# Rotating the place of the weight pairs inside their buffers, in a two-layer encoder trunk

## The chip, the cores and the metric

The kernel runs on one core of a Trainium2 chip. The metric is the device time of one execution in microseconds (us). Two runs of the kernel before took 1237.33 and 1236.85 us; their median is 1237.09 us.

## The reference

The kernel computes a small encoder trunk of depth 2 on one sequence of 512 frames with 1024 features, in float32:

```python
for layer in range(DEPTH):
    mod = c_act @ mod_w[layer] + mod_b[layer]
    sh1, sc1, g1, sh2, sc2, g2 = jnp.split(mod, N_MOD, axis=-1)
    u = modulate(rms_norm(h, norm_mix[layer]), sh1, sc1)
    if layer < N_A_LAYERS:
        mix = hgrn2_mixer(u, a_w_in[layer], a_w_out[layer], lower_bounds[layer], a_out_norm[layer])
    else:
        j = layer - N_A_LAYERS
        mix = chunk_band_attention(u, k_pad, v_pad, b_w_q[j], b_w_o[j], b_rel_bias[j])
    h = h + g1[:, None, :] * mix
    u = modulate(rms_norm(h, norm_ffn[layer]), sh2, sc2)
    h = h + g2[:, None, :] * swiglu(u, ffn_w_in[layer], ffn_w_out[layer])
    if layer == N_A_LAYERS - 1:
        k_pad, v_pad = shared_kv(h, c_act, kv_norm, kv_mod_w, kv_mod_b, kv_w)
return rms_norm(h, final_norm)
```

Layer 0 mixes with a gated linear recurrence of 8 heads, layer 1 with a band attention of 16 heads; each layer ends with a feed-forward part, `swiglu(u) = (silu(u @ gate) * (u @ up)) @ w_out`, whose inner width is 2816. All large products have a weight matrix from memory on one side and the activations of the 512 frames on the other.

## The kernel before, in words

**Precision by pairs.** A large product is done in the reduced format `float32r`. Each operand is split into a high part (a rounded copy, made by ScalarE) and a low part (the operand less its high part, made by VectorE), and three matmuls are added up in PSUM: high by high, high weight by low input, low weight by high input. `mm3` (L187) does this for one block of 128 by 128 weights, L190 to L192. TensorE loads the 128 weight columns first (LDWEIGHTS, "PEld" in the profile, while the matmul before is still running) and then streams the 512 or 256 columns of the other operand past them. So there is one weight load for each matmul.

**The weights' way.** `load` (L146) reads a block of weights, 1024 floats in each of 128 partitions, by a DMA on the SP queue into a buffer of the tag `raw`. `fetch` and `split` (L123) make the pair `wh`, `wl` out of it, one block ahead of its use. The pool `wp` has three buffers for each tag, and a buffer of the tags `wh` and `wl` is as long as the longest tile that asks for one: 64 + 1024 floats, 4352 bytes. `SHIFT` (L54) is the 64. Four blocks (the two weights of tile 3 of each feed-forward part) get their low part from ScalarE and an adding DMA on the POOL queue instead (L130, L131).

**Where the operands lie.** In the kernel before, a pair made by `split` starts at the head of its buffers, and so do the eight first pairs made by `high` (L653). In the allocation of the kernel before, the heads of all six `wh` and `wl` buffers lie 192 bytes above a multiple of 256 (the first at byte 66,240), and so do the split activations (`u0h` at 20,928, the inputs of the fast tiles at 128,960 or 120,768, with every later tile a multiple of 256 bytes further). So a weight row (512 bytes) that is loaded for `mm3` starts at distance 0 modulo 256 bytes from the row that is streaming. "Distance" below is this one: of the weights loaded from the row that streams, modulo 256 bytes.

**The fast tiles.** In both feed-forward parts the first four of the 22 inner tiles go through `mm3` with 512 streamed columns. The other 18 (`fast_tiles`, L515) are done by a scheme with seven products of half-sized blocks in place of eight, on sums and differences of weights and inputs. `prepare` makes four pairs for each tile, with `halves` (L520): the pairs of `w1`, `w2`, `w3` hold two operands of 512 floats each, `w4` holds one. `product` (L553) then does 4 by 3 matmuls of 256 streamed columns, at L558 (high, high), L559 (high weight, low input) and L560 (low weight, high input). That is 84 matmuls for a tile and 3,024 for 36 tiles. These pairs do not start at the head:

```python
wh, wl = (wp.tile([P, SHIFT + D], F32R, tag="w" + x, name=f"{key}_{x}")[:, NEAR:NEAR + 4 * n_ * P]
          .rearrange("p (i j c) -> p i j c", i=n_, j=4) for x in "hl")
```

`NEAR` is 48 floats, so they lie at distance 192.

**The other weight products.** Outside the fast tiles, 8 first pairs with 18 matmuls each, 82 pairs with 24, and the 16 output rows of the feed-forward parts (three pairs, 22 blocks, 66 matmuls each) make 144 + 1,968 + 1,056 = 3,168 matmuls. The very last row streams its 512 frames as two halves of 256 columns, so there are 3,102 of 512 and 132 of 256 columns. All of them load at distance 0. (In the value projections, L213 to L215, the weights are streamed and the activations are loaded.)

**Order.** Each engine works its queue in order; semaphores are set by the tile framework. TensorE's order is the order of the program: the weight products fill in around the small products of the recurrence and of the attention. The change does not touch any of this.

Of the kernel before, what the change touches and what calls it, by code (L numbers as in the profile page):

```python
# [10 lines left out]
F32R = mybir.dt.float32r  # L11
# [4 lines left out]
P = 128  # L16
D = 1024
# [33 lines left out]

SHIFT, NEAR = 64, 48  # L54


V1_AFTER, CREDIT, RATES = 1, 3.0, (3.5, 16, 2.0, 56, 1.5)
# [12 lines left out]
def trunk(ctx: ExitStack, tc: tile.TileContext, d, out):  # L70
# [4 lines left out]
    wp = ctx.enter_context(tc.tile_pool(name="wp", bufs=3))  # L75
# [3 lines left out]
    def bank(name):  # L79
        return pp.tile([P, S], F32, tag="ps", name=name)  # L80
# [6 lines left out]
    h = [cst.tile([P, S], F32, tag=f"h{j}", name=f"h{j}") for j in range(KT)]  # L87
# [28 lines left out]
    V.tensor_mul(cact, cols[:, C_C:C_C + KT], csig)  # L116


    def by_transfer(key):

        return key[0] in [f"f{layer}" for layer in FAST] and key[1] == PLAIN - 1

    def split(raw, nk, n, nm, tag, key):  # L123
        wh = wp.tile([P, nk, n], F32R, tag=tag + "h", name=f"{nm}_h")
        wl = wp.tile([P, nk, n], F32R, tag=tag + "l", name=f"{nm}_l")
        A.activation(wh, raw, AF.Copy)  # L126

        state.pop("meanwhile", lambda: None)()
        if by_transfer(key):
            A.activation(wl, raw, AF.Copy, scale=-1.0)  # L130
            G.dma_start(out=wl, in_=raw, accum_op=ALU.add)  # L131
        else:
            low = V.tensor_sub(wl, raw, wh)  # L133
            if key[0] in ("av", "g", "zf", "q", "ao") or key[1] == "o":
                state["mods_after"] = low
        return wh, wl
# [2 lines left out]
    plan = weight_plan(d)  # L139
    ready = {}  # L140
    shifts, partial = {}, {}
    state = {"loaded": 0, "split": 0, "used": 0}
    raws = {}
    LOAD_AHEAD, SPLIT_AHEAD = 2, 1

# [8 lines left out]
    def fetch(i, ahead):  # L154
        load(i + LOAD_AHEAD + 1)
        if i + ahead + 1 < len(plan) and by_transfer(plan[i + ahead + 1][0]):
            ahead += 1
        while state["split"] < min(i + ahead + 1, len(plan)) and plan[state["split"]][0][-1] not in ("c1", "c2"):
            key, _, nk, n = plan[state["split"]]
            nm = "_".join(str(x) for x in key)  # L160
            raw = raws.pop(key)
            ready[key] = split(raw, nk, n, nm, "w", key)
            if key in shifts:

                sh = shifts[key]
                pa = sm.tile([P, S], F32, tag="et", name=f"wsh_{nm}", bufs=2)[:, 0:P]
                V.tensor_scalar_mul(pa, raw[:, 0, :], sh[:, 0:1])
                for kt in range(1, nk):
                    V.scalar_tensor_tensor(pa, raw[:, kt, :], sh[:, kt:kt + 1], pa, op0=ALU.mult, op1=ALU.add)
                partial[key] = pa  # L170
            state["split"] += 1

    def weight(key, ahead=SPLIT_AHEAD):
        assert plan[state["used"]][0] == key, (plan[state["used"]][0], key)
        fetch(state["used"], ahead)
        state["used"] += 1
        return ready.pop(key)

    def take(key):

        assert plan[state["used"]][0] == key, (plan[state["used"]][0], key)
        load(state["used"] + LOAD_AHEAD + 1)
        state["used"] += 1
        state["split"] = state["used"]
        return raws.pop(key)
# [329 lines left out]
    def fast_tiles(fp, nm, slot, activated, kept, side):  # L515

        H = S // 2
        ops = {}

        def halves(key, raw, n_):  # L520
            wh, wl = (wp.tile([P, SHIFT + D], F32R, tag="w" + x, name=f"{key}_{x}")[:, NEAR:NEAR + 4 * n_ * P]
                      .rearrange("p (i j c) -> p i j c", i=n_, j=4) for x in "hl")
            A.activation(wh, raw, AF.Copy)  # L523
            V.tensor_sub(wl, raw, wh)  # L524
            return [(wh[:, i], wl[:, i]) for i in range(n_)]

        def prepare(n):

            m = f"{nm}_{n}"
            c1 = take((nm, n, "c1")).rearrange("p (o j) c -> p o j c", o=2)  # L530
            c2 = take((nm, n, "c2")).rearrange("p (o j) c -> p o j c", o=2)
            x1 = fp.tile([P, 2, 4, P], F32, tag="x1", name=f"{m}_x1")
            x2 = fp.tile([P, 2, 4, P], F32, tag="x2", name=f"{m}_x2")
            b11, b21, b22, b12 = c1[:, 0], c1[:, 1], c2[:, 0], c2[:, 1]
            t2, t1, t3, t4 = x1[:, 0], x1[:, 1], x2[:, 0], x2[:, 1]
            ops[n, 1], ops[n, 2] = halves(f"{m}_w1", c1, 2)
            V.tensor_sub(t1, b12, b11)
            V.tensor_sub(t2, b22, t1)
            yield
            ops[n, 6], ops[n, 5] = halves(f"{m}_w2", x1, 2)  # L540
            V.tensor_sub(t3, b22, b12)
            V.tensor_sub(t4, b21, t2)
            yield
            ops[n, 7], ops[n, 4] = halves(f"{m}_w3", x2, 2)
            yield
            ops[n, 3], = halves(f"{m}_w4", c2[:, 0:1], 1)
            yield

        def stream():
            for n in range(PLAIN, FT):  # L550
                yield from prepare(n)

        def product(n, i, ps, s, start, stop):  # L553
            wh, wl = ops.pop((n, i))
            for j in range(4):
                uh, ul = slot(j, s)
                f = start and j == 0
                T.matmul(ps, wh[:, j, :], uh, start=f, stop=False, skip_group_check=True)  # L558
                T.matmul(ps, wh[:, j, :], ul, start=False, stop=False, skip_group_check=True)  # L559
                T.matmul(ps, wl[:, j, :], uh, start=False, stop=stop and j == 3, skip_group_check=True)  # L560

        chunks = stream()
        done = {"n": 0}

        def ahead(upto):
            while done["n"] < upto and next(chunks, chunks) is not chunks:
                done["n"] += 1

        AHEAD = 2
        for i, n in enumerate(range(PLAIN, FT)):  # L570
            at = activated(n)
            r1, r2, r3 = (bank(f"{nm}_r{q}_{n}")[:, 0:H] for q in (1, 2, 3))
            pu = sm.tile([P, 2, H], F32, tag="ut", name=f"{nm}_pu{n}", bufs=2)
            qu = sm.tile([P, 2, H], F32, tag="et", name=f"{nm}_qu{n}", bufs=2)
            p1, u2, p5, u3 = pu[:, 0, :], pu[:, 1, :], qu[:, 0, :], qu[:, 1, :]
            row1, row2 = at[:, H:S], at[:, 0:H]

            ahead(4 * i + 1 + AHEAD)
            product(n, 1, r1, 1, True, True)
            A.activation(p1, r1, AF.Copy)  # L580
            product(n, 5, r2, 4, True, True)
            A.activation(p5, r2, AF.Copy)
            ahead(4 * i + 2 + AHEAD)
            product(n, 6, r1, 5, False, True)
            A.activation(u2, r1, AF.Copy)
            product(n, 2, r3, 3, True, True)
            V.tensor_add(p1, r3, p1)
            A.activation(p1, p1, AF.Silu)
            ahead(4 * i + 3 + AHEAD)
            product(n, 7, r1, 6, False, True)  # L590
            A.activation(u3, r1, AF.Copy)
            ahead(4 * i + 4 + AHEAD)
            product(n, 3, r2, 7, False, True)
            V.tensor_add(row2, u3, p5)
            V.tensor_add(row1, r2, u2)
            V.tensor_mul(row1, row1, p1)
            product(n, 4, r1, 2, False, True)
            A.activation(p5, r1, AF.Silu)
            last = V.tensor_mul(row2, row2, p5)
            kept(n, at)  # L600
            if i % 3:
                state["mods_after"] = last
                next(side, None)
        state["mods_after"] = last
        fetch(state["used"] - 1, 1)
# [11 lines left out]
    first = [bank(f"first{i}") for i in range(6)]  # L617
    fraw, mrow, wfs, u, sqs, a1 = {}, {}, {}, {}, {}, []
# [32 lines left out]
        return r  # L651

    def high(j):  # L653
        wfs[j] = [wp.tile([P, 6, P], F32R, tag="w" + x, name=f"first{j}_{x}") for x in "hl"]
        A.activation(wfs[j][0], fraw[j], AF.Copy)

    def low(j):
# [312 lines left out]
    with tc.manual_schedule():  # L970
# [21 lines left out]
        A.activation(crow[:, S:S + 256], pcs[1][:, 0:256], AF.Copy)  # L992
        V.tensor_copy(crow[:, S + 256:D], pcs[1][:, 256:S])
        high(0)
        a1.append(mod_entry(0, 1))
        rounded(0)
# [126 lines left out]
    for n in range(2):  # L1123
        w, ps = weight(("ao", n)), bank(f"ao_{n}")
# [11 lines left out]
    for n in range(KT):  # L1136
        if n < len(part):
            w, ps = part[n]
# [36 lines left out]
    with tc.tile_pool(name="attn", bufs=1) as ap:  # L1175
# [146 lines left out]
        for k in range(len(units) + LAG2 + 1):  # L1322
            if k < len(units):
                hd, i = units[k]
# [20 lines left out]
        for n in range(KT):  # L1345
            if n < len(part):
                w, ps = part[n]
# [219 lines left out]
```

## Time and profile before

| what | value |
|---|---|
| median of 2 runs | 1237.09 us |
| span of the profiled execution | 1235.1 us |
| TensorE matmuls busy | 1219.8 us, 8548 instructions |
| TensorE weight loads busy | 1061.0 us, 8548 instructions |
| VectorE busy | 987.8 us |
| ScalarE busy | 648.8 us |
| matmuls of the fast tiles | 3 groups of 1008 |

The span runs from the first to the last instruction of the profiled execution. No time of its own beside the span is shown for that execution; the median of the runs is 2.0 us above its span, and this is taken for what lies around it. A matmul's duration in the profile is longer than the distance to the next one's start, because matmuls overlap in the array. What a matmul costs in a dense stretch is the time from its start to the start of the next.

### The profile page before, as it was taken

To read this page: it belongs to the slowest core of one execution; us is meant where nothing else is said; L and a number is where in the kernel's file an instruction comes from. 1 tells how busy PE (TensorE), PEld (TensorE's weight loads), DVE (VectorE), ACT (ScalarE), POOL (GpSimd) and SP (SyncE) were. 2 spreads that over 40 slices of the span, in tenths; PEclk is the share of its full clock that TensorE was granted. 3 is DMA by queue.
4 is the path that set the end of the run, shared out by engine and by line. 5 is a ranking of instruction groups with operands and counts; after the bars stand their busy time and mean duration, and the time that the engine had idled before them with its cause. 6 is when DMAs were issued, how large, how long until landed. Compare 5 with 4: busy or idle time off the path is not lost.

```text
span 1235.1 us, 21555 instructions
## 1 busy us (share of the span) xinstructions
PE 1219.8 (99%) x8548; PEld 1061.0 (86%) x8548; DVE 987.8 (80%) x1769; ACT 648.8 (53%) x1157; POOL 21.4 (2%) x29
## 2 busy tenths in 40 slices
PE   8999999999999999999999999999999999999997
PEld 7888788778899999988888877777889999998887
DVE  8996878887989999987669878996788999984333
ACT  6455446444655555742228566675465555563221
POOL 0100000000000000000000000000000000000000
PEclk9999999999999999999999999999999999999999
DMA  9642345553434444568752444532243444342331
GB/s 353 254 133 88 123 170 164 172 192 106 123 114 140 137 137 140 164 210 277 233 168 71 140 147 152 172 100 68 69 134 106 137 137 137 103 129 94 96 92 68
DMA packets 52532, 177.55 MB, mean 144 GB/s; under 512 B 5968, under 2 KB 8400, under 8 KB 52432
## 3 DMA queue, kind: packets, MB, share of 16 engines
q1 hardware_dynamic: 51856, 174.08, 43.1%
q0 software_dynamic: 576, 2.10, 1.0%
q8 instruction: 67, 1.10, 0.4%
q14 instruction: 33, 0.27, 0.1%
HBM read 171.96 MB, written 2.10 MB: 141 GB/s over the span
## 4 chain that ended last, share of the span: by engine, by line
PE 90%; DVE 5%; ACT 3%; issue 1%; DMA 1%; POOL 0%; DVEq 0%; POOLq 0%; ACTq 0%
PE f_r L560 10%; PE f_r L559 9%; PE f_r L558 9%; PE f_o L191 6%; PE f_o L192 6%; PE f_o L190 6%; PE f L190 2%; PE f L192 2%; PE f L191 2%; PE o L858 1%; PE bo L1270 1%; PE bo L190 1%; PE av L213 1%; PE bo L192 1%; PE bo L191 1%; PE ao L192 1%
## 5 line engine op out<-in xcount | busy, mean ns | idle before, releaser
L560 PE MATMUL f_r<-f_h,f_w_l 128*128 128x256 f32 x1008 | 282.3, 280 | 0.0
L558 PE MATMUL f_r<-f_h,f_w_h 128*128 128x256 f32 x1008 | 281.2, 279 | 0.0
L559 PE MATMUL f_r<-f_l,f_w_h 128*128 128x256 f32 x1008 | 281.2, 279 | 0.0
L559 PEld LDWEIGHTS f_r<-f_l,f_w_h 128*128 128x128 f32 x1008 | 189.5, 188 | 0.1
L560 PEld LDWEIGHTS f_r<-f_h,f_w_l 128*128 128x128 f32 x1008 | 189.2, 188 | 0.0
L558 PEld LDWEIGHTS f_r<-f_h,f_w_h 128*128 128x128 f32 x1008 | 188.5, 187 | 0.1
L191 PE MATMUL f_o<-f_p,f_o_h 128*128 128x512 f32 (+1 forms) x374 | 141.1, 377 | 0.3 <-DVE f_p L475 0.3
L192 PE MATMUL f_o<-f_p,f_o_l 128*128 128x512 f32 (+1 forms) x374 | 141.2, 378 | 0.0
L190 PE MATMUL f_o<-f_p,f_o_h 128*128 128x512 f32 (+1 forms) x374 | 140.8, 377 | 0.0
L126 ACT ACTIVATE f_o_h<-r_f_o 128x1024 fp32r<-128x1024 f32 (+1 forms) x48 | 46.8, 987 | 131.9 <-PE f_o L191 101.3
L340 DVE SCALAR_TENSOR_TENSOR mw<-mw,crow 128x1024 f32<-128x1024 f32 x96 | 115.4, 1218 | 0.7 <-DMA mw<-in_modw 0.6
L133 DVE TENSOR_TENSOR f_o_l<-r_f_o,f_o_h 128x1024 fp32r<-128x1024 f32 (+1 forms) x48 | 54.1, 1132 | 68.0 <-ACT f_o_h L126 60.4
L523 ACT ACTIVATE f_w_h<-f_x 128x1024 fp32r<-128x1024 f32 x72 | 76.5, 1063 | 49.1 <-PE f_r L559 42.0
L524 DVE TENSOR_TENSOR f_w_l<-f_x,f_w_h 128x1024 fp32r<-128x1024 f32 x72 | 88.0, 1225 | 8.7 <-ACT f_w_h L523 4.0
L523 ACT ACTIVATE f_w_h<-r_f_c 128x1024 fp32r<-128x1024 f32 x72 | 61.1, 848 | 49.5 <-PE f_r L559 48.1
L192 PEld LDWEIGHTS f_o<-f_p,f_o_l 128*128 128x128 f32 x374 | 70.3, 188 | 14.1 <-DVE f_o_l L133 1.4
L191 PEld LDWEIGHTS f_o<-f_p,f_o_h 128*128 128x128 f32 x374 | 70.4, 188 | 13.5 <-DVE f_p L475 0.7
L190 PEld LDWEIGHTS f_o<-f_p,f_o_h 128*128 128x128 f32 x374 | 70.4, 188 | 12.9
L524 DVE TENSOR_TENSOR f_w_l<-r_f_c,f_w_h 128x1024 fp32r<-128x1024 f32 x72 | 68.6, 952 | 7.7 <-ACT f_w_h L523 7.5
L1245 ACT ACTIVATE sb<-sb,st 128x128 f32<-128x128 f32 (+1 forms) x64 | 35.8, 560 | 29.9 <-DVE st L1244 29.4
L761 DVE TENSOR_TENSOR kq<-kq,t 128x1024 f32<-128x1024 f32 x28 | 34.2, 1220 | 5.2 <-PE fine L785 2.7
L192 PE MATMUL f<-f_h,f_l 128*128 128x512 f32 x96 | 36.9, 391 | 0.0
(401 smaller groups left out, 2706.3 us busy)
## 6 DMA issues: line engine op xcount, KB each, us to landing
mw<-in_modw SPq DMA_DIRECT2D x96, 512.0 KB, 4.2
r_f_c<-in_ffn_in SPq DMA_DIRECT2D x72, 512.0 KB, 3.5
r_f_o<-in_ffn_out SPq DMA_DIRECT2D x32, 512.0 KB, 3.6
mrow<-in_modw SPq DMA_DIRECT2D x16, 512.0 KB, 8.2
r_f<-in_ffn_in SPq DMA_DIRECT2D x16, 512.0 KB, 3.5
r_f_o<-in_ffn_out SPq DMA_DIRECT2D x16, 384.0 KB, 3.4
r_av<-in_a_v SPq DMA_DIRECT2D x8, 512.0 KB, 4.1
r_g<-in_a_g SPq DMA_DIRECT2D x8, 512.0 KB, 3.3
```

The source lines that it names most:

```text
L126: A.activation(wh, raw, AF.Copy)
L133: low = V.tensor_sub(wl, raw, wh)
L190: T.matmul(ps, wh[:, kt, :], uh, start=start, stop=False)
L191: T.matmul(ps, wh[:, kt, :], ul, start=False, stop=False)
L192: T.matmul(ps, wl[:, kt, :], uh, start=False, stop=stop)
L340: V.scalar_tensor_tensor(mw, mw, 1.0, crow, op0=ALU.mult, op1=ALU.mult, accum_out=raw[:, j:j + 1])
L523: A.activation(wh, raw, AF.Copy)
L524: V.tensor_sub(wl, raw, wh)
L558: T.matmul(ps, wh[:, j, :], uh, start=f, stop=False, skip_group_check=True)
L559: T.matmul(ps, wh[:, j, :], ul, start=False, stop=False, skip_group_check=True)
L560: T.matmul(ps, wl[:, j, :], uh, start=False, stop=stop and j == 3, skip_group_check=True)
L1245: A.activation(s[:, 0:n], s[:, 0:n], AF.Exp, bias=st[:, 1:2], accum_out=st[:, 2:3])
```

## The change

All pairs of weights, from `split`, from `halves` and from `high`, now come from one helper, `placed`. It takes a whole buffer of 64 + 1024 floats and hands out a part of it that starts 0, 8, 16, ... 56 floats behind the head: 0 to 224 bytes in steps of 32. A counter goes up by one for each half of a pair, so the high and the low part of one pair lie at the same distance, and the next pair lies 32 bytes further, in the order in which pairs are made. The number of instructions, their order, the sizes of the buffers and the waits are as before.

```diff
-SHIFT, NEAR = 64, 48
+SHIFT, STEP = 64, 8
...
+    def placed(name, tag, nk, n):
+        t = wp.tile([P, SHIFT + D], F32R, tag=tag, name=name)
+        at = STEP * (state["placed"] // 2 % (SHIFT // STEP))
+        state["placed"] += 1
+        return t[:, at:at + nk * n].rearrange("p (k c) -> p k c", k=nk)
...
     def split(raw, nk, n, nm, tag, key):
-        wh = wp.tile([P, nk, n], F32R, tag=tag + "h", name=f"{nm}_h")
-        wl = wp.tile([P, nk, n], F32R, tag=tag + "l", name=f"{nm}_l")
+        wh, wl = (placed(f"{nm}_{x}", tag + x, nk, n) for x in "hl")
...
-    state = {"loaded": 0, "split": 0, "used": 0}
+    state = {"loaded": 0, "split": 0, "used": 0, "placed": 0}
...
         def halves(key, raw, n_):
-            wh, wl = (wp.tile([P, SHIFT + D], F32R, tag="w" + x, name=f"{key}_{x}")[:, NEAR:NEAR + 4 * n_ * P]
-                      .rearrange("p (i j c) -> p i j c", i=n_, j=4) for x in "hl")
+            wh, wl = (placed(f"{key}_{x}", "w" + x, 4 * n_, P).rearrange("p (i j) c -> p i j c", i=n_) for x in "hl")
...
     def high(j):
-        wfs[j] = [wp.tile([P, 6, P], F32R, tag="w" + x, name=f"first{j}_{x}") for x in "hl"]
+        wfs[j] = [placed(f"first{j}_{x}", "w" + x, 6, P) for x in "hl"]
```

Fifty pairs are made before the first fast tile of layer 0 (8 first, 8 and 10 and 8 and 8 of the mixer, 8 of the plain tiles) and 186 before that of layer 1, both 2 more than a multiple of 8. So in both layers the fast tiles alternate between the distances 64, 96, 128, 160 and 192, 224, 0, 32 for their four pairs. The first three pairs of a tile serve 24 matmuls each and the fourth 12, so of the 3,024 matmuls 432 load at each of 0, 64, 96, 128, 192 and 224 bytes, and 216 at each of 32 and 160. The other weight products spread evenly over the eight.

## The prediction

> **What bounds the kernel now.** I read the page first: the busy times, then the chain that ended last.
>
> ```profile
> span 1235.1 us, 21555 instructions
> ...
> PE 1219.8 (99%) x8548; PEld 1061.0 (86%) x8548; DVE 987.8 (80%) x1769; ACT 648.8 (53%) x1157; POOL 21.4 (2%) x29
> ...
> PEclk9999999999999999999999999999999999999999
> ...
> PE 90%; DVE 5%; ACT 3%; issue 1%; DMA 1%; POOL 0%; DVEq 0%; POOLq 0%; ACTq 0%
> ```
>
> TensorE works all the time at full granted clock, and nine tenths of the chain are its matmuls. The time is the sum of start-to-start distances of matmuls, so the change can act only through these, or through another engine made so slow that it becomes late. Next the groups of instructions, kept apart by shape, for the matmuls that the change touches:
>
> ```profile
> L560 PE MATMUL f_r<-f_h,f_w_l 128*128 128x256 f32 x1008 | 282.3, 280 | 0.0
> L558 PE MATMUL f_r<-f_h,f_w_h 128*128 128x256 f32 x1008 | 281.2, 279 | 0.0
> L559 PE MATMUL f_r<-f_l,f_w_h 128*128 128x256 f32 x1008 | 281.2, 279 | 0.0
> ...
> L191 PE MATMUL f_o<-f_p,f_o_h 128*128 128x512 f32 x330 | 128.6, 390 | 0.3 <-DVE f_p L475 0.3
> ...
> L191 PE MATMUL f_o<-f_p,f_o_h 128*128 128x256 f32 x44 | 12.5, 285 | 0.0
> ```
>
> The same shape, 256 streamed columns, lasts 279 ns in the fast tiles, where weights lie at distance 192, and 285 ns in the last output row, where they lie at distance 0. To see what that is worth I took the order of time on TensorE in three dense stretches, first and last of equal steps:
>
> ```profile
> 341.82 0.28 PE L560 MATMUL f_r<-f_h,f_w_l 128*128 128x256 f32 x1
> ...
> 348.89 0.28 PE L560 MATMUL f_r<-f_h,f_w_l 128*128 128x256 f32 x1
> ```
>
> ```profile
> 1209.79 0.28 PE L190 MATMUL f_o<-f_p,f_o_h 128*128 128x256 f32 x1
> ...
> 1218.43 0.28 PE L190 MATMUL f_o<-f_p,f_o_h 128*128 128x256 f32 x1
> ```
>
> ```profile
> 599.71 0.39 PE L191 MATMUL f_o<-f_p,f_o_h 128*128 128x512 f32 x1
> ...
> 605.83 0.39 PE L191 MATMUL f_o<-f_p,f_o_h 128*128 128x512 f32 x1
> ```
>
> Sixty steps of 256 columns at distance 192 take 7.07 us, 117.8 ns each. Seventy-two steps of 256 columns at distance 0 take 8.64 us, 120.0 ns each. Twenty-seven steps of 512 columns at distance 0 take 6.12 us, 226.7 ns each. At distance 0, 256 more columns cost 226.7 - 120.0 = 106.7 ns, so 256 columns alone take 106.7 ns, and 13.3 ns come on top of each matmul whatever its length: the price of its weight load at distance 0. At distance 192 that price is 117.8 - 106.7 = 11.1 ns. So the trace shows one effect of place, of 2.2 ns, at two of the eight distances.
>
> **The change, part by part.** Nothing is removed or added: instructions, waits, DMAs and their order are the same. What moves is the distance.
>
> The fast tiles, 3,024 matmuls: 432 go to distance 0 and pay 2.2 ns more, 0.95 us. 432 stay at 192 and change by nothing. The other 2,160 load at distances that no row shows. The nearest rows are the two that I have; I take the middle between them, 118.9 ns, as nothing draws it to either: 2,160 x 1.1 ns = 2.4 us. Between the ends, like 192 or like 0, this is 0 to 4.75 us. Beyond both ends, a gain or a loss is not excluded; the rivals price it.
>
> The 3,102 matmuls of 512 columns: 388 stay at distance 0. 2,714 leave it. Two places in the trace have a 512-column matmul while a load at distance 192 runs, the last before the fast tiles of each layer:
>
> ```profile
> 339.95 0.39 PE L192 MATMUL f<-f_h,f_l 128*128 128x512 f32 x1
> 340.17 0.28 PE L558 MATMUL f_r<-f_h,f_w_h 128*128 128x256 f32 x1
> ```
>
> ```profile
> 925.48 0.39 PE L192 MATMUL f<-f_h,f_l 128*128 128x512 f32 x1
> 925.71 0.28 PE L558 MATMUL f_r<-f_h,f_w_h 128*128 128x256 f32 x1
> ```
>
> They take 0.22 and 0.23 us, mean 0.225 against 0.2267, which with times rounded to 10 ns speaks for a small gain, not for a large one. The ends are no gain and the 2.2 ns of the shorter matmuls, 0 to 6.0 us. I take 0.5 ns, nearer to no gain, since the mean over the seven distances lies between none (if like 0) and what 192 gives, which those two rows hold small: -1.4 us. The 132 half-width matmuls of the last row gain 1.1 ns in seven of eight: -0.1 us.
>
> The writers of the pairs, ScalarE and VectorE, now write and read at other places:
>
> ```profile
> L523 ACT ACTIVATE f_w_h<-f_x 128x1024 fp32r<-128x1024 f32 x72 | 76.5, 1063 | 49.1 <-PE f_r L559 42.0 <-PE f L191 4.0 <-DVE f_x L538 3.1
> ...
> L126 ACT ACTIVATE f_o_h<-r_f_o 128x1024 fp32r<-128x1024 f32 x32 | 33.9, 1060 | 95.1 <-PE f_o L191 64.6 <-issue 27.3 <-PE f_r L559 2.9
> ```
>
> ```profile
> L524 DVE TENSOR_TENSOR f_w_l<-f_x,f_w_h 128x1024 fp32r<-128x1024 f32 x72 | 88.0, 1225 | 8.7 <-ACT f_w_h L523 4.0
> ...
> L133 DVE TENSOR_TENSOR f_o_l<-r_f_o,f_o_h 128x1024 fp32r<-128x1024 f32 x32 | 39.2, 1224 | 60.7 <-ACT f_o_h L126 60.4
> ...
> L524 DVE TENSOR_TENSOR f_w_l<-r_f_c,f_w_h 128x512 fp32r<-128x512 f32 x36 | 24.6, 684 | 1.0 <-ACT f_w_h L523 1.0
> ```
>
> At 192 and at 0 they last the same, 1063 against 1060 ns and 1225 against 1224 ns. I cost them at nothing. ScalarE's cover is that it waits for TensorE to free a buffer before it writes. VectorE's is thinner, seen in the stretches of time:
>
> ```profile
> 342.00:425.00 83.00, 83.00 (x707) 83.00 (x707) 76.56 (x118) 48.16 (x84) 0.00 (x0) 1.00 0.38 123
> ```
>
> The columns are TensorE, weight loads, VectorE, ScalarE, POOL. VectorE is busy for 76.56 of 83 us, so 8% is free in the fast tiles; if it were used up, VectorE would be late and each us over it would count.
>
> Four pairs have a low part by DMA from the POOL queue; they now land 0 or 32 bytes from the head:
>
> ```profile
> f_l<-r_f POOLq DMA_DIRECT2D x4, 512.0 KB, 5.0
> ```
>
> ```profile
>   DMA f_l<-r_f: 0.4, 2
> ```
>
> The second row, from the view of the tile, says that TensorE waited for them twice, 0.4 us in all. There is no cover left, so a slower landing would count twice (the second block in each layer). At distance 32 nothing is shown; from none to a tenth of the 5.0 us each, 0 to 1 us. I take none, as the first of each two stays at the head.
>
> Sum: 0.95 + 2.4 - 1.4 - 0.1 = +1.9 us. The span goes from 1235.1 to 1237.0 us. The median of the runs stands 2.0 us above the span, and with that I forecast 1239.0 us. With the ends of the terms it is from 1237.1 + 0.95 - 6.0 - 0.25 = 1231.8 to 1237.1 + 0.95 + 4.75 = 1242.8 us.
>
> **The rivals.**
>
> One or more distances clear the load (faster). The 13.3 and 11.1 ns may be a meeting of the two reads that some distance avoids wholly. One such distance saves 11.1 x 432 = 4.8 us in the fast tiles and 13.3 x 388 = 5.2 us elsewhere, 10 us: 1229 us. Two give 1219, three 1209 us; more than that VectorE's 8% would cap in the fast tiles. For it: place has an effect at all. Against: a move of 192 of 256 bytes took off only a sixth, and the same in all rows. The Trainium skill, "TensorE: Matmul & The Clock Gate", section "Back-to-back issue gap", gives a matmul N/2.4 + 2.5 ns, 109.2 and 215.8 ns for 256 and 512 columns; the trace has 117.8 to 120.0 and 226.7, and an estimate by the page would make a cleared distance worth 8 us instead of 10.
>
> Nothing moves. The 2.2 ns may belong to the last row, which streams half rows and fills half a bank, not to distance; then the time stays 1237.1 us. Against: rows of both kinds stream 256 columns with the same three operands. The rule beside this: the same page, section "Step-by-step: what each phase is for", says that TensorE has two independent read ports, so that loading weights takes no read bandwidth from the running matmul; by that place is of no effect. The trace shows 13.3 ns a load and a difference between two places, which speaks against it.
>
> Some distances meet worse (slower than before). In the fast tiles and elsewhere, 2,160 and 2,327 matmuls go to distances without a row; each ns on all of them costs 4.5 us. It decides against the forecast above distance 0's price, and by over 2% (24.7 us) where those six cost 5.5 ns more than before, a load price of 17 to 19 ns in place of 11 to 13. As an end: if loads were not hidden at all, their 188 ns would stand in place of 117.8 ns,
>
> ```profile
> L558 PEld LDWEIGHTS f_r<-f_h,f_w_h 128*128 128x128 f32 x1008 | 188.5, 187 | 0.1
> ```
>
> 30 us for each distance of 432. Against: distance 0, where both reads start at the same place, should be among the worst.
>
> VectorE becomes the bound. If odd multiples of 32 bytes slowed L524 by a third, the 8% would be gone. For each tile, L524 takes three times 1.225 us and once 0.684, 4.4 us of the 84 x 117.8 ns = 9.9 us of TensorE; a third is 1.5 us against 0.8 free, 0.7 us x 36 = 25 us. Against: no row of VectorE shows an effect of place.
>
> **How the numbers follow.** Forecast 52%, 1232 to 1243 us, at 1239. Nothing moves 14%. One distance clear 12%, two or more 6%. Worse distances 10%, half of them up to 1246. VectorE 3%, the DMA 3% (1240 us). For 8 in 10 the range is 1229 to 1246 us: it adds one clear distance below and 0.8 ns on the six distances above. A change of 2% is about what a measurement of this kernel can tell from none. Faster by over 2% needs three clear distances, 5%; slower by over 2%, 5%; within, 90%.
>
> **What would show it.** In the changed profile the fast tiles should step in blocks: 120.0 ns a matmul at distance 0, 117.8 at 192, values between in other blocks, no change within a block of one pair. The 512-column rows should step by 226.7 ns in one pair of eight and by up to 2.2 ns less in others. L523 and L524 should keep 1063 and 1225 ns. Wrong would be blocks near 107 or above 125 ns, or idle time of TensorE ended by L524.

## The result, and the profile after

The changed kernel takes 1248.32 us (1248.08 and 1248.55) against 1237.09 us: 1.0089 times as long, 95% interval 1.0073 to 1.0106. That is 11.2 us slower; the forecast was 1239.0 us, and the range ended at 1246.

The page of the changed kernel (all lines of the code have moved down by four or five):

```profile
span 1246.2 us, 21555 instructions
...
PE 1232.4 (99%) x8548; PEld 1062.7 (85%) x8548; DVE 988.6 (79%) x1769; ACT 648.7 (52%) x1157; POOL 20.7 (2%) x29
...
PEclk9999999999999999999999999999999999999999
...
PE 93%; DVE 3%; ACT 2%; issue 1%; DMA 0%; POOL 0%; DVEq 0%; POOLq 0%; ACTq 0%
```

The span is 11.1 us longer. TensorE is busy for 12.6 us more with the same 8548 instructions, at the same granted clock, and the other engines for what they were. Nothing new waits; the matmuls themselves follow one another more slowly. Four of the groups, kept apart by shape:

```profile
L562 PE MATMUL f_r<-f_h,f_w_h 128*128 128x256 f32 x1008 | 282.8, 281 | 0.0
...
L196 PE MATMUL f_o<-f_p,f_o_h 128*128 128x512 f32 x330 | 130.3, 395 | 0.1
```

```profile
L527 ACT ACTIVATE f_w_h<-f_x 128x1024 fp32r<-128x1024 f32 x72 | 76.4, 1061 | 51.5 <-PE f_r L563 44.1
L528 DVE TENSOR_TENSOR f_w_l<-f_x,f_w_h 128x1024 fp32r<-128x1024 f32 x72 | 88.0, 1224 | 9.3 <-ACT f_w_h L527 3.7
```

The writers are untouched (1061 for 1063 ns, 1224 for 1225). The matmuls of 512 columns have gone from 390 to 395 ns, those of the fast tiles only from 279 to 281. The order of time on TensorE says where the 11.1 us lie. First matmuls of stages, before:

```profile
518.36 0.40 PE L190 MATMUL f_o<-f_p,f_o_h 128*128 128x512 f32 x1
...
638.92 0.39 PE L190 MATMUL e_k<-us2h,k_h 128*128 128x512 f32 x1
...
1103.78 0.40 PE L190 MATMUL f_o<-f_p,f_o_h 128*128 128x512 f32 x1
```

and after:

```profile
344.38 0.28 PE L562 MATMUL f_r<-f_h,f_w_h 128*128 128x256 f32 x1
...
522.82 0.40 PE L195 MATMUL f_o<-f_p,f_o_h 128*128 128x512 f32 x1
...
645.72 0.40 PE L195 MATMUL e_k<-us2h,k_h 128*128 128x512 f32 x1
...
934.32 0.28 PE L562 MATMUL f_r<-f_h,f_w_h 128*128 128x256 f32 x1
...
1112.75 0.40 PE L195 MATMUL f_o<-f_p,f_o_h 128*128 128x512 f32 x1
```

With the two first fast matmuls of before that the prediction shows (340.17 and 925.71) and the two spans, the stages are:

| stage | before, us | after, us | more |
|---|---|---|---|
| to the first fast tile | 340.17 | 344.38 | 4.21 |
| fast tiles, layer 0 | 178.19 | 178.44 | 0.25 |
| output rows, layer 0 | 120.56 | 122.90 | 2.34 |
| to the fast tiles of layer 1 | 286.79 | 288.60 | 1.81 |
| fast tiles, layer 1 | 178.07 | 178.43 | 0.36 |
| output rows, layer 1, and the end | 131.32 | 133.45 | 2.13 |

The fast tiles give 0.6 us of the 11.1; the other 10.5 us lie where matmuls stream 512 columns. (The 3,102 steps of 512 columns alone add up to 728.0 us before and 738.5 us after.) In the output rows of layer 0, where before every step is 226.7 ns from the third row on, the order of time of the changed kernel shows one block for each pair. First and last of like steps in a block at distance 192, then one at 0, then one at 64:

```profile
584.60 0.40 PE L195 MATMUL f_o<-f_p,f_o_h 128*128 128x512 f32 x1
...
585.30 0.39 PE L195 MATMUL f_o<-f_p,f_o_h 128*128 128x512 f32 x1
585.52 0.39 PE L196 MATMUL f_o<-f_p,f_o_h 128*128 128x512 f32 x1
...
589.64 0.39 PE L196 MATMUL f_o<-f_p,f_o_h 128*128 128x512 f32 x1
...
595.47 0.39 PE L197 MATMUL f_o<-f_p,f_o_l 128*128 128x512 f32 x1
...
599.33 0.39 PE L196 MATMUL f_o<-f_p,f_o_h 128*128 128x512 f32 x1
...
605.15 0.39 PE L197 MATMUL f_o<-f_p,f_o_l 128*128 128x512 f32 x1
...
610.51 0.40 PE L196 MATMUL f_o<-f_p,f_o_h 128*128 128x512 f32 x1
```

At distance 0, 17 steps take 3.86 us, 227 ns each. At 64, 23 steps take 5.36 us, 233 ns. At 192, 22 steps take 5.04 us, 229 ns. One of the steps at 192, from 585.30 to 585.52, is 0.22 us. It stands between others of 0.23 and 0.24: within a block the steps are not equal but repeat a short pattern (by the unrounded starts: 229, 231, 226 ns at 192; 231, 236 at 64; 229, 238 at 128; a constant 226.7 only at 0). Over all 512-column matmuls of the trace (those of the value projections too, where the pair is streamed), with the steps left out that hold a wait, the mean step is 228 ns at distance 0, 230 at 192, and 232.5 to 233.6 at the six others. The head, which I had taken for one of the worse places, is the best of the eight.

The fast tiles hold the other surprise. Distance 64 comes twice in the even tiles, with the same pair from the same buffer: once behind a block at 0, and once behind a block at 96. Tile 14 of layer 0:

```profile
443.51 0.28 PE L562 MATMUL f_r<-f_h,f_w_h 128*128 128x256 f32 x1
...
444.69 0.28 PE L563 MATMUL f_r<-f_l,f_w_h 128*128 128x256 f32 x1
...
447.62 0.28 PE L564 MATMUL f_r<-f_h,f_w_l 128*128 128x256 f32 x1
...
448.87 0.28 PE L563 MATMUL f_r<-f_l,f_w_h 128*128 128x256 f32 x1
```

Ten steps take 1.18 us, 118 ns; then eleven take 1.25 us, 113.6 ns. (By the unrounded starts 117.8 and 113.3, and so in all 18 even tiles of the two layers.) The distance alone does not fix the step.

### The profile page after: what moved, and what is told of

Its sections match the earlier page's. It is cut to its first block, busy times and chain, and to the rows that moved or that the text cites. A ratio compares the mean times of both kernels' runs of the same rounds, so it can differ in the third digit from the quotient of the medians.

```text
span 1246.2 us, 21555 instructions
## 1 busy us (share of the span) xinstructions
PE 1232.4 (99%) x8548; PEld 1062.7 (85%) x8548; DVE 988.6 (79%) x1769; ACT 648.7 (52%) x1157; POOL 20.7 (2%) x29
## 4 chain that ended last, share of the span: by engine, by line
PE 93%; DVE 3%; ACT 2%; issue 1%; DMA 0%; POOL 0%; DVEq 0%; POOLq 0%; ACTq 0%
PE f_r L562 10%; PE f_r L563 10%; PE f_r L564 9%; PE f_o L196 6%; PE f_o L197 6%; PE f_o L195 6%; PE f L195 2%; PE f L196 2%; PE f L197 2%; PE o L862 1%; PE av L218 1%; PE bo L195 1%; PE bv L218 1%; PE bv L219 1%; PE bv L220 1%; PE ao L197 1%
## 5 line engine op out<-in xcount | busy, mean ns | idle before, releaser
L196 PE MATMUL f_o<-f_p,f_o_h 128*128 128x512 f32 (+1 forms) x374 | 142.7, 382 | 0.1
L195 PE MATMUL f_o<-f_p,f_o_h 128*128 128x512 f32 (+1 forms) x374 | 142.2, 381 | 0.0
L527 ACT ACTIVATE f_w_h<-f_x 128x1024 fp32r<-128x1024 f32 x72 | 76.4, 1061 | 51.5 <-PE f_r L563 44.1
L528 DVE TENSOR_TENSOR f_w_l<-f_x,f_w_h 128x1024 fp32r<-128x1024 f32 x72 | 88.0, 1224 | 9.3 <-ACT f_w_h L527 3.7
L527 ACT ACTIVATE f_w_h<-r_f_c 128x1024 fp32r<-128x1024 f32 x72 | 61.1, 848 | 48.6 <-PE f_r L563 47.2
L528 DVE TENSOR_TENSOR f_w_l<-r_f_c,f_w_h 128x1024 fp32r<-128x1024 f32 x72 | 68.6, 953 | 9.8 <-ACT f_w_h L527 9.8
L196 PE MATMUL f<-f_l,f_h 128*128 128x512 f32 x96 | 37.2, 394 | 0.0
```

What stands on the lines that cost most here:

```text
L195: T.matmul(ps, wh[:, kt, :], uh, start=start, stop=False)
L196: T.matmul(ps, wh[:, kt, :], ul, start=False, stop=False)
```

## The experiments

All twelve kernels compute the full result. The diffs are against the changed kernel; its one line in `placed` that sets the place is replaced. Distances are as in the prediction, modulo 256 bytes.

**Which matmuls lose: the fast tiles alone, and the others alone.**

```diff
-        at = STEP * (state["placed"] // 2 % (SHIFT // STEP))
+        fast = re.match(r"f[01]_\d+_w\d_", name)
+        at = STEP * (state["placed"] // 2 % (SHIFT // STEP)) if fast else 0
```

> The pairs of the fast tiles rotate over the eight distances as in the changed kernel; all other pairs stay at the head of their buffers. Theory A (the loss is in the 512-column matmuls outside the fast tiles, whose steps grew from 226.7 ns to 229 to 234 ns at every distance but 0): about 1237.7 us, 1236.5 to 1239. Rival B (the loss is in the fast tiles, or evenly on both): 1242 us or more. Rival C (the writers of the pairs cost it): 1242 us, as about half of the pairs rotate.

Measured: 1237.76 us, ratio 1.0005 (0.9995 to 1.0014). Then the other half of the change:

```diff
+        at = 48 if fast else STEP * (state["placed"] // 2 % (SHIFT // STEP))
```

> The other half of the change: the fast pairs stay at 192 bytes, all others rotate. Theory A: 1246 to 1249 us, nearly all of the 11.2 us, with the steps of the 512-column matmuls as in the changed kernel. Rivals B and C: 1242 us or less.

Measured: 1247.36 us, ratio 1.0083 (1.0067 to 1.0099). The rotation costs nothing measurable in the fast tiles; nearly all of the loss, 10.3 us, is made by the pairs outside them.

**Place in the buffer, address, or distance.** The kernel before is built again through `placed`, so that every pair has its old place in its buffer, but 64 unused bytes lie ahead of the pool of the weights (and 192 behind it). Only the distance to the streaming rows changes: 192 becomes 0 and 0 becomes 64.

```diff
+        at = 48 if fast else 0
...
+    gap1 = ctx.enter_context(tc.tile_pool(name="gap1", bufs=1))
+    V_gap1 = gap1.tile([P, 16], F32, tag="gap1", name="gap1")
...
     wp = ctx.enter_context(tc.tile_pool(name="wp", bufs=3))
...
```

> The kernel before with two unused tiles, 64 bytes ahead of the pool of the weights and 192 bytes behind it: every weight buffer moves up by 64 bytes, all that is streamed stays. Within their buffers the pairs start where they did before. Theory A says that the distance between the loaded and the streamed row counts: the 512-column steps go to about 233 ns (distance 64), the fast tiles to 120 ns (distance 0), 1237 + 15 + 7 = 1259 us, 1253 to 1262. Rival D (the place in the buffer counts): 1237 us.

Measured: 1255.74 us, ratio 1.0150 (1.0129 to 1.0172). Two stretches of 74 and 80 us, one in the fast tiles and one in the output rows, first of the kernel before and then of this one; the columns are the length, TensorE's busy time with its matmuls, the clock, and the DMA:

```profile
426.00:500.00 74.00, 74.00 (x630) 1.00 0.47 150
555.00:635.00 80.00, 80.00 (x354) 1.00 0.73 239
```

```profile
426.00:500.00 74.00, 74.00 (x619) 1.00 0.40 137
555.00:635.00 80.00, 80.00 (x344) 1.00 0.72 239
```

That is 74 / 619 = 119.5 ns and 80 / 344 = 232.6 ns, against 117.5 and 226.0 ns before (a count takes in a matmul at either edge, so each value is a little low). These are the values of distances 0 and 64, with no pair moved within its buffer. The counterpart moves everything by 64 bytes, weights and streamed rows alike (the unused 64 bytes lie ahead of the first pool):

> The kernel before with one unused tile of 64 bytes ahead of everything: weights and streamed rows move up together by 64 bytes, distances stay. Theory A: no change, 1236 to 1238 us, steps of 226.7 and 117.8 ns. Rival E (the address as such counts, modulo 256 bytes): the 512-column steps change, 1242 us or more.

Measured: 1236.91 us, ratio 0.9997 (0.9988 to 1.0007). What counts is where the loaded row lies relative to the streaming one, not where either lies.

**What each distance costs.** Two scans give each fast tile and each output row one distance, the first in steps of 16 bytes (ascending through layer 0, descending through layer 1), the second in steps of 4:

```diff
+        m = re.match(r"f([01])_(\d+)_w\d_", name)
+        o = re.match(r"f([01])_o_(\d+)_", name)
+        at = 0
+        if m:
+            tile_n = int(m[2]) - PLAIN
+            at = FINEST * (tile_n if m[1] == "0" else 16 - tile_n) % SPAN
+        elif o:
+            at = FINEST * (max(int(o[2]), 1) - 1 + 8 * int(o[1])) % SPAN
```

`FINEST` is 4 floats in the first and 1 float in the second scan, `SPAN` 64 floats.

> A look at steady distances: all other pairs at the head; each fast tile has one distance for its four pairs, 16 bytes further from tile to tile (rising in layer 0, falling in layer 1), and each output row of the feed-forward parts has one, 16 bytes further from row to row. Theory F (a step depends on the distance and on the steps before it, so that a run of steps at one distance falls into a repeating pattern): at multiples of 32 the 512-column rows repeat the patterns of the changed kernel (0: 226.7; 32: 233; 64: 233.5; 128: 233.5; 192: 229), odd multiples of 16 lie between their neighbours; the fast tiles show more than one pattern for a distance, by whether they come from above or from below. Rival G (one step has one price for each distance): the same mean for a distance from both sides. Time by both 1240 to 1243 us.

Measured, in one run: 1243.63 us. The order of time on TensorE, the fast tile at 64 in layer 0 and in layer 1:

```profile
380.50 0.28 PE L571 MATMUL f_r<-f_h,f_w_h 128*128 128x256 f32 x1
...
389.80 0.28 PE L572 MATMUL f_r<-f_l,f_w_h 128*128 128x256 f32 x1
...
1048.74 0.28 PE L571 MATMUL f_r<-f_h,f_w_h 128*128 128x256 f32 x1
...
1058.40 0.28 PE L572 MATMUL f_r<-f_l,f_w_h 128*128 128x256 f32 x1
```

82 steps each: 9.30 us are 113.4 ns behind 48, and 9.66 us are 117.8 ns behind 80. So a whole tile keeps the value that it was entered with, and the theory that each distance has one value falls. Distances 128 and 144 too had two values each (118.7 and 120.0, 118.3 and 119.9 ns). One thing came out against theory F's expectation: the output row at 80 steps by 231.9 ns, not between its neighbours at 64 and 96 (233.3 and 234.2 ns).

> The same with 4 bytes for 16: 0 to 60 bytes. Theory H (reads go in pieces of 32 bytes): flat from 0 to 28 bytes and from 32 to 60, 512-column steps of 226.7 and of about 233 ns. Rival I (pieces of 16 bytes or less, or of 4): a change at 16, or at each step. Time 1238 to 1243 us.

Measured, in one run: 1242.49 us. Four bytes are enough to change a tile: in layer 0 the tile at 48 steps by 117.8 ns, the tile at 52 by 113.3, the tile at 56 by 117.8. That ends theory H. And the output rows have two values as well. Distance 16 in the first scan, entered from 0:

```profile
550.33 0.39 PE L204 MATMUL f_o<-f_p,f_o_h 128*128 128x512 f32 x1
...
564.83 0.39 PE L205 MATMUL f_o<-f_p,f_o_h 128*128 128x512 f32 x1
```

and in the second, entered from 12:

```profile
595.20 0.40 PE L204 MATMUL f_o<-f_p,f_o_h 128*128 128x512 f32 x1
...
610.13 0.40 PE L205 MATMUL f_o<-f_p,f_o_h 128*128 128x512 f32 x1
```

64 steps each: 226.6 against 233.3 ns.

A third scan takes the multiples of 4 that were left, 68 to 252, and other distances for the output rows. `FINE_PLACES` lists the former in floats, `ROW_PLACES` the latter in bytes:

```diff
+            at = FINE_PLACES[int(m[2]) - PLAIN + 18 * int(m[1])]
...
+            at = ROW_PLACES[int(o[1])][int(o[2])] // 4
```

> A scan of the distances that no run has shown yet: the fast tiles at the multiples of 4 from 68 to 252 that are no multiples of 16, one pair for each, and the output rows of 512 columns at 240, 60, 248, 112, 244, 120, 252, 104, 0, 52, 20, 88, 24 and 72. Theory I (each step of 4 bytes changes how the load and the streamed rows meet): fast steps spread over 113 to 122 ns with no order by 16 or 32 bytes, and the 512-column rows between 226.7 and 235 ns. Rival: beyond 64 bytes only multiples of 16 differ, and neighbours within 16 bytes agree within 1 ns. Time 1239 to 1244 us by either, since the mean of the fast steps stays near 118 and only a quarter of the rows of 512 columns is moved off the head. It is looked at for a step under 113.3 ns in the fast tiles and under 226.7 ns in the rows.

Measured, in one run: 1243.51 us. The order of time for the fast tiles at 76 and at 108:

```profile
360.56 0.28 PE L572 MATMUL f_r<-f_h,f_w_h 128*128 128x256 f32 x1
...
369.87 0.28 PE L573 MATMUL f_r<-f_l,f_w_h 128*128 128x256 f32 x1
...
419.64 0.28 PE L572 MATMUL f_r<-f_h,f_w_h 128*128 128x256 f32 x1
...
429.66 0.29 PE L573 MATMUL f_r<-f_l,f_w_h 128*128 128x256 f32 x1
```

82 steps each, 113.5 and 122.2 ns, and the neighbour of 76 at 72 has 118.3: no order by 16 or 32 bytes. No block in any of the three scans settled below 113.3 ns for 256 columns or 226.7 ns for 512, the one twice the other.

**The history.** First all fast pairs at 64 and the rest at the head:

```diff
+        at = 16 if fast else 0
```

> The kernel before with the fast pairs at 64 in place of 192 bytes. In the changed kernel the first pair of every second fast tile lies at 64; its steps were 117.7 ns where it came after distance 0 and 113.3 ns where it came after distance 96. Theory F: one of the two for all 3,024 steps; the fast tiles come after distance 0 here, so 117.7 ns and 1236.8 us; if a disturbance leads to the other, 113.3 ns and 1224 us. Rival G: the mean of 115.6 ns, 1230 us.

Measured: 1237.32 us, ratio 1.0001 (0.9992 to 1.0011). The fast tiles are entered from distance 0, and all 36 stay at the slow value for 64:

```profile
426.00:500.00 74.00, 74.00 (x631) 1.00 0.46 152
```

74 / 631 = 117.3 ns (again a little low). Then the same, with one pair in each layer, the first of the first fast tile, at 96:

```diff
+        at = (24 if "_4_w1_" in name else 16) if fast else 0
```

> As the one before, but the very first fast pair of each layer lies at 96 bytes, all later ones at 64. Theory F: 113.3 ns for all steps, 1224 us, 1222 to 1227. Rival G: 1230 us, as two pairs of 144 change nothing.

Measured: 1228.01 us, ratio 0.9926 (0.9911 to 0.9941). The same stretch, and two of 11 us in layer 1:

```profile
426.00:500.00 74.00, 73.98 (x653) 1.00 0.44 143
...
1003.00:1014.00 11.00, 11.00 (x100) 1.00 0.57 178
1018.00:1029.00 11.00, 11.00 (x95) 1.00 0.28 97
```

653 matmuls in place of 631. The pair at 96 is used in two blocks of 12. Behind the first the steps at 64 are 117.8 ns still; behind the second they are 113.3, and they hold for tile after tile, long after that pair is gone. So it isn't the distance just before that decides, either. In layer 1 they hold up to tile 14 only. The order of time there, with the weight loads:

```profile
1016.36 0.28 PE L566 MATMUL f_r<-f_l,f_w_h 128*128 128x256 f32 x1
...
1016.64 0.19 PEld L567 LDWEIGHTS f_r<-f_h,f_w_l 128*128 128x128 f32 x1 [0.21 <-DVE f_w_l L531]
1016.65 0.39 PE L567 MATMUL f_r<-f_h,f_w_l 128*128 128x256 f32 x1
```

A load waits 0.21 us for VectorE, and behind it the steps are 117.8 ns to the end of the layer. If the wait did it, it cost not 0.2 us but, with nearly 8 tiles of 84 matmuls by 4.4 ns, 3 us, and without it the time would be near 1225 us, inside the 1222 to 1227 expected. That the wait is the cause rests on this one place, where the steps change right behind it: a wait as long in the same tile of layer 0 left them at 113.3 ns.

Distance 52 had come out at 113.3 ns from both sides in the scan, so it was tried for all fast pairs:

```diff
+        at = 13 if fast else 0
```

> All pairs of the fast tiles at distance 52, the pairs outside the fast tiles at the head as before. In the scan by 4 bytes distance 52 had steps of 113.33 ns in the fast tiles both when it was entered from 48 and when it was entered from 56. If the steps hold that value whatever ran before (theory F, with 52 as a place that has one pattern only): 3,024 fast matmuls at 113.3 instead of 117.8 ns, 13.6 us less, about 1224 us (1222 to 1227), and no tile of 117.8 ns. If 52 too has a second pattern (theory F, with a second pattern met in some tiles), between 1224 and 1237 us, with tiles at another value in the trace. If VectorE, which was busy 76.6 of 83 us in the fast tiles, cannot follow the shorter steps: waits of TensorE on VectorE in the fast tiles and a time nearer 1230 us.

Measured: 1244.09 us, ratio 1.0057 (1.0044 to 1.0071), a miss:

```profile
426.00:500.00 74.00, 74.00 (x619) 1.00 0.44 146
```

All tiles step by 120.0 ns. 52 has a second pattern too, and entry from 0 leads into it. The next kernel differs from this in one fast pair of each layer (of 72; its expectation miscounts them as 54), which lies 4 bytes nearer the head:

```diff
+        at = (12 if "_4_w1_" in name else 13) if fast else 0
```

> As the kernel with all fast pairs at distance 52, which ran at 1244.1 us with steps of 120.0 ns throughout, but the first pair of fast tile 4 of each layer lies at distance 48. One pair of 54 in each layer is moved, by 4 bytes. In the scan by 4 bytes the block at 52 came behind the block at 48 and had 113.33 ns. If the distance just before decides which pattern a block falls into: 113.3 ns from then on, 3,000 times 6.7 ns or 20 us less than 1244.1, about 1224 us. If the whole history decides, down to where the pattern stood when the distance changed, 120.0 ns may stay and the time with it: 1244 us. If the time depended on the distance of each matmul alone, 1244 us as well and the block at 48 would be the only one with other steps.

Measured, in one run: 1224.13 us, 20 us less. Two stretches, the second with VectorE's busy time in the third place:

```profile
426.00:500.00 74.00, 73.98 (x652) 1.00 0.42 142
```

```profile
342.00:425.00 83.00, 83.00 (x734) 83.00 (x733) 78.65 (x123) 50.40 (x87) 0.00 (x0) 1.00 0.40 134
```

From the first block at 52 on, the steps at 52 are 113.3 ns in all 36 tiles. This is the clearest of the runs: for 71 of the 72 fast pairs of a layer, and for all others, every place, length and order is the same as in the kernel of 1244 us. VectorE is busy for 78.65 of 83 us, so little is left to win here before it becomes the bound.

Last, the kernel with 64 behind 96, and the first pair of tile 15 at 96 too, to enter the pattern anew behind the wait:

```diff
+        at = (24 if re.search("_(4|15)_w1_", name) else 16) if fast else 0
```

> As the kernel with the first fast pair at distance 96 and the others at 64 (1228.0 us), but the first pair of fast tile 15 lies at 96 too, so that a pattern lost in tile 14 of the second layer is entered anew. If a load at 96 always leads into the pattern of 113.33 ns: tiles 15 to 21 of the second layer step by 113.3 instead of 117.8 ns, 7 tiles of 84 matmuls by 4.4 ns, 2.6 us less, at the price of two pairs of 24 loads at 118 ns, 0.2 us: about 1225.6 us (1224.5 to 1227). If the entry depends on where the pattern stood: the first layer, which comes to 96 from 113.33 ns and not from 118, may fall to 117.8 ns behind it, 2.6 us more: 1228 to 1231 us.

Measured: 1225.66 us, ratio 0.9905 (0.9889 to 0.9922). It beats both kernels of the case, by 0.95% and 1.8%. The time is the one that the first theory gives, but the trace shows that it came another way. The wait in tile 14 of layer 1 is there again, and behind it, still ahead of tile 15:

```profile
1017.44 0.19 PEld L567 LDWEIGHTS f_r<-f_h,f_w_l 128*128 128x128 f32 x1 [0.22 <-DVE f_w_l L531]
1017.45 0.38 PE L567 MATMUL f_r<-f_h,f_w_l 128*128 128x256 f32 x1
...
1018.36 0.28 PE L565 MATMUL f_r<-f_h,f_w_h 128*128 128x256 f32 x1
...
1025.28 0.28 PE L566 MATMUL f_r<-f_l,f_w_h 128*128 128x256 f32 x1
```

61 steps take 6.92 us, 113.4 ns each. The pattern was not lost, so tile 15 had nothing to mend, and that the forecast time came out is luck. Its blocks at 96, now entered from 113.3 ns, step by 120.2 ns in both layers and not by 117.4 as in tile 4, and the steps at 64 behind them are 113.3 again, so the second theory falls. Such a wait, of 0.21 or 0.22 us in tile 14, stands six times in the traces of this kernel, of the one with 96 in tile 4 alone and of the one with 48 ahead of 52; behind one of the six the steps changed. Why that one is open.

## Why the prediction was wrong, point by point

**The step that failed** is the term of the 512-column matmuls, "I take 0.5 ns, nearer to no gain ... -1.4 us", with ends of 0 and -6.0. It measured about +10.5 us (table of stages), and some 10 us with nothing else changed (1247.36 us). Two things were wrong in it. It read a steady value out of one step: the 0.22 and 0.23 us at the two boundaries are both 226 ns by the unrounded starts, the lowest value of the pattern 229, 231, 226 that distance 192 settles into, whose mean is above 226.7, not below. And the term had no end on the side of a loss; that was left to a rival, with the argument against it that distance 0, "where both reads start at the same place, should be among the worst". No row stood behind that sentence. The rows in hand had distance 0 as the worse of two places for 256 columns; for 512 it is the best of the eight.

**The decomposition** of a step into 106.7 ns for 256 columns and a fixed price of 13.3 ns a load subtracted steps of two patterns from each other. The lowest steps met are 113.3 and 226.7 ns, in the ratio of the columns, so no fixed price shows in them. By these runs a cleared distance is worth at most 117.8 - 113.3 = 4.5 ns a fast matmul, 2 us for each 432, and nothing in the 512-column matmuls, not the 10 us of the rival.

**The fast tiles** were forecast at +3.35 us and gave +0.6 (and no difference within the interval in the run that rotates them alone). The blocks at 0 and 192 came as said, near 120 and 118 ns in the trace. The middle taken for the other six, 118.9 ns, was too high: they average 117.7 ns, since 64 (115.9, with 113.3 behind 96) and 96 (117.2) fell below both ends, while 160, 32 and 128 (119.7, 118.6 and 118.4) lay between them. So the small sum is a balance of gains and losses.

**What was costed at nothing** was nothing: L527 and L528 kept their times, and no wait on VectorE appeared in the fast tiles. VectorE's thin cover showed only in the faster kernels, in the waits of tile 14.

**The rivals.** The one that came true is "some distances meet worse": its 10% rested on the sentence quoted above, and in the sum it was at work in the 512-column matmuls alone, 4 ns on their mean step (227.8 to 232.0 ns over all of them in the two traces, steps with a wait left out). "Nothing moves" falls with the experiments on distance. Moving nothing but the relative place by 64 bytes took the time from 1237 to 1255.7 us. The Trainium skill, "TensorE: Matmul & The Clock Gate", section "Step-by-step: what each phase is for", has two independent read ports, by which the load takes nothing from the stream; these runs disagree with it as far as place goes.

**What stays open.** That the step depends on the place of the loaded rows relative to the streamed ones, and on the steps before, in patterns that lock in, is shown. That it is the two reads that meet is the nearest reading of this, not shown; nor is how they meet, why 4 bytes matter, or when a wait changes the pattern; no run here looks inside a step, and the value of a distance could not be told ahead, only scanned.

## What to carry to other kernels

Where TensorE's matmuls are dense, take the step from start to start over a whole block, not from one step at a boundary, and compare it with the lowest that any block of that length reaches. The distance between the loaded weights and the streamed rows, modulo 256 bytes here, is worth up to 8% of a step (113.3 to 122.2 ns), and it must be measured in the order in which the kernel runs it, since the same distance can settle at two values. Spreading weights over many places averages over good and bad ones; one good place, entered the right way, gave 1% here.

## What the runs showed that was not expected

A stretch of matmuls has a memory. At distance 64 it steps by 113.3 or 117.8 ns, at 52 by 113.3 or 120.0 ns, and keeps the one it was entered with over more than a thousand matmuls; one pair moved by 4 bytes in each layer decided 20 us of 1244. Behind a wait of 0.21 us it went from one value to the other once; behind five such waits it did not. And the lowest steps of 256 and 512 columns, 113.3 and 226.7 ns, are in the ratio of the columns, while the weight load of 188 ns beside them takes longer than the shorter one.
